# Input laid out turned for the start of a two-layer kernel, with contiguous weight blocks and more value tiles

## The chip, the cores and the metric

The kernel runs on one core of one Trainium2 chip. The metric is the device time of one execution in microseconds (us), as the median of several executions. The engines are TensorE (PE in the profile, PEld for its loading of weights), VectorE (DVE, `V` in the code), ScalarE (ACT, `S`), GpSimd (POOL, `G`) and SyncE (SP), which issues most of the DMA transfers (`nc.sync`). An engine name with a q behind it is that engine's sequencer.

## The reference

A batch of one, 256 tokens, width 2048, float32. A first layer (RWKV-7: five mixed inputs, four 2048x2048 products, a scan over 32 heads of 64, an output product), then a second (sparse attention with compressed, selected and window branches), each behind an rmsnorm, and a last norm. What the change touches is computed here:

```python
def rmsnorm(x, g):
    xf = x.astype(jnp.float32)
    y = xf * lax.rsqrt(jnp.mean(xf * xf, axis=-1, keepdims=True) + NORM_EPS)
    return (y * g.astype(jnp.float32)).astype(x.dtype)
...
    xx = token_shift(u) - u
    mixed = u[None] + xx[None] * mu[:, None, None, :]
    rkvz = jnp.einsum('nbtd,nde->nbte', mixed[:4], w_rkvz)
...
    def step(S, inp):
        r_t, w_t, k_t, v_t, a_t, b_t = inp
        sa = jnp.einsum('bhvk,bhk->bhv', S, a_t)
        S = S * w_t[:, :, None, :] + sa[..., None] * b_t[:, :, None, :] + v_t[..., None] * k_t[:, :, None, :]
        return S, jnp.einsum('bhvk,bhk->bhv', S, r_t)
```

Here u is the normed x of the first layer.

## The kernel before

**Precision and weights.** Each float32 operand of a large product is split into a high part and a low part (the rest), and three products make one. Weights arrive in pieces of 512 KB (`wraw`, five buffers, issued on SP in L179); ScalarE writes the high part (L213) and VectorE subtracts for the low part (L192), a few units ahead of TensorE (class `Weights`: `ensure`, `high`, `low`). While `W.hold` is set, low parts are written one at a time by `W.low(1)`. Weights for v, z and the outputs are loaded by rows of 512 columns or more (`rows`), those for r, k and the gate of the second layer by blocks of 128 columns (`cols128`, L293), whose rows in memory are 512 bytes long.

**Inputs.** The mixed inputs have the width on partitions: 16 blocks of 128 by 256 tokens. `xn` holds the normed x with a zero column ahead of the first token, `xx` the difference to the token before; `mixed_in` (L432) makes one mixed block of them on VectorE, `split_into` (L426) its high part on ScalarE and its low part on VectorE.

**Start (L346 to L505).** x is loaded on SP by tokens, two tiles of 128 tokens by 2048, in five pieces with three small parameter loads between them. ScalarE and VectorE square and sum them (`square`), VectorE and POOL make the reciprocal norm (`rstd0`), VectorE multiplies x by it (`scale`), TensorE turns the blocks (`turn_half`, `turn_x`), ScalarE multiplies by the gain and copies to `xn`, and VectorE or POOL makes `xx` (`norm_x`). The parameter rows are turned on TensorE as well. `keep_warm(n)` has TensorE multiply ones by ones, with no use of the result; `WARM` says how often at each place. `manual_schedule` holds the engines to the order of the program there. Blocks 2 to 15 are prepared by a generator (`prep`, `mixgen_v`), and another (`mixgen`) makes the inputs for w, a, z, k and r; both are pumped while the products run.

**Products of the first layer.** `phase_v` runs the v product and the two narrow products for w and a over all blocks, four blocks at a time; `store_v` (L626) copies its result through `vst` tiles on ScalarE and stores it to memory. Then come z, sixteen blocks of k with their own chain on all engines, and the inverse of small triangular matrices, made in pieces on VectorE, ScalarE and POOL (L822) and stored to `tnd` and `yvd`.

**Scan (L988 to L1545).** Eight pairs U of heads are worked through beside the r product and the first output products. A planner (`Deal`) lists every step with its engine, an estimated duration, what it needs and a lag, computes due times, and issues the steps in the order that it finds; `("at", n)` is a time of n us in its plan before which a step isn't placed. The engines and SP keep this order. Steps used here: `a` and `y` load pieces of the inverse (`load_a`, `load_y`, which fills `Yb`) on POOL's DMA queue; `v` loads the values into `uv`; `gb` loads the gain and bias of the group norm; `ars` are decay products on POOL; `G` (L1062) is the first PE step that needs `a` and `y` of a pair.

**Second layer.** `rstd` gives `RS`, the reciprocal norm per token; at the start of the attention it is spread over columns and turned into `RST` (L1754). `phase_q` splits turned queries into `qh` and `ql` (L1792, L1793).

## Time and profile before

| | us |
|---|---|
| median of 3 runs | 1132.98 |
| lowest and highest | 1128.69, 1133.59 |
| the profiled execution | 1135.73 |
| its span, first to last instruction | 1133.7 |
| TensorE busy in it | 1101.0 |
| VectorE busy | 860.5 |
| ScalarE busy | 713.5 |
| POOL busy | 378.0 |

The profile is of one execution. A row of its timeline has the start, the time taken, the engine, the line of the kernel, the operation, the tile written and the tiles read, the count, and in brackets the idle time before it with what ended it. A row of a group has line, engine, operation, tiles, shapes and count, then busy time and the mean in ns of one, then idle time before it and what ended that. A row of waits has who waited for whom, the sum, how often, and the longest. Matmuls are pipelined, so a busy TensorE need not be at its peak.

### The profile page before, as it was taken

Reading aid. Unit: us, or ns where it says so; the run is one execution under the profiler, and the core shown is the slowest. Engines: PE = TensorE matmul, PEld = TensorE weight load, DVE = VectorE, ACT = ScalarE, POOL = GpSimd, SP = SyncE. Lnnn points to the kernel's source line nnn. Section 1 sums busy time; section 2 is a strip of 40 time slices with the busy share of each in tenths; the row PEclk is TensorE's granted clock in tenths of the full one; section 3 lists DMA queues with packets and bytes.
Section 4 is the critical chain, followed back from the end, with each engine's and each line's share of the span. In section 5 each row is a group of like instructions: output and inputs, shape, how many; then the busy total and the mean of one; then the engine's idle time right before and its main releaser. Section 6 shows DMA issues by size and latency. Waiting matters only on the chain.

```text
span 1133.7 us, 24534 instructions
## 1 busy us (share of the span) xinstructions
PE 1101.0 (97%) x8880; PEld 935.3 (83%) x8880; DVE 860.5 (76%) x1783; ACT 713.5 (63%) x1700; POOL 378.0 (33%) x487
## 2 busy tenths in 40 slices
PE   7999999999999999999999999999999999999997
PEld 7778899987788777877788888787889988888786
DVE  6998976789869797677567776764576888988564
ACT  5667688867665356655556766664666666666553
POOL 1400057755384546661010010101334435362212
PEclk9999999999999999999999999999999999999999
DMA  6568888976999968865457658585645453848562
GB/s 221 172 194 221 246 220 245 258 204 210 263 293 273 229 159 244 201 186 156 133 177 250 205 167 290 164 282 167 188 146 159 124 140 102 210 120 276 160 190 104
DMA packets 239033, 225.35 MB, mean 199 GB/s; under 512 B 58053, under 2 KB 185333, under 8 KB 238912
## 3 DMA queue, kind: packets, MB, share of 16 engines
q1 hardware_dynamic: 233472, 216.65, 65.8%
q0 software_dynamic: 5440, 7.14, 2.3%
q8 instruction: 70, 1.15, 0.5%
q14 instruction: 51, 0.42, 0.1%
HBM read 200.48 MB, written 23.10 MB: 197 GB/s over the span
## 4 chain that ended last, share of the span: by engine, by line
PE 73%; DVE 13%; DMA 4%; issue 4%; ACT 3%; POOL 2%; SPq 0%; ACTq 0%; POOLq 0%; DVEq 0%
PE bank L589 11%; PE bank L591 11%; PE bank L588 11%; PE bank L1348 5%; DVE wlo L192 5%; PE bank L613 4%; PE bank L614 2%; PE bank L607 2%; PE bank L1351 2%; PE bank L244 2%; PE bank L608 2%; PE bank L609 2%; PE pair L1370 2%; ACT whi L213 1%; PE pair L1372 1%
## 5 line engine op out<-in xcount | busy, mean ns | idle before, releaser
L192 DVE TENSOR_TENSOR wlo<-wraw,whi 128x512 fp32r<-128x512 f32 (+2 forms) x616 | 444.3, 738 | 164.1 <-ACT whi L213 161.6
L213 ACT ACTIVATE whi<-wraw 128x512 fp32r<-128x512 f32 (+2 forms) x661 | 397.9, 619 | 221.4 <-PE bank L591 79.7
L589 PE MATMUL bank<-wlo,mx 128*128 128x512 f32 (+3 forms) x576 | 216.1, 377 | 3.6 <-DVE wlo L192 2.7
L591 PE MATMUL bank<-whi,mx 128*128 128x512 f32 (+3 forms) x576 | 214.2, 374 | 0.0
L588 PE MATMUL bank<-whi,mx 128*128 128x512 f32 (+3 forms) x576 | 186.9, 376 | 1.8 <-ACT mx L428 0.9
L589 PEld LDWEIGHTS bank<-wlo,mx 128*128 128x128 f32 x576 | 108.3, 188 | 22.7 <-DVE wlo L192 5.4
L588 PEld LDWEIGHTS bank<-whi,mx 128*128 128x128 f32 x576 | 107.6, 188 | 19.1 <-ACT mx L1937 1.2
L591 PEld LDWEIGHTS bank<-whi,mx 128*128 128x128 f32 x576 | 108.3, 188 | 16.3 <-POOL mx L1938 0.4
L1348 PE MATMUL bank<-mx,whi 128*128 128x512 f32 x256 | 102.1, 430 | 0.0
L192 POOL TENSOR_TENSOR wlo<-wraw,whi 128x512 fp32r<-128x512 f32 (+2 forms) x48 | 63.1, 1316 | 110.6 <-ACT whi L213 88.7
L613 PE MATMUL bank<-mx,whi 128*128 128x512 f32 x240 | 86.8, 398 | 0.0
L607 PE MATMUL bank<-mx,whi 128*128 128x256 f32 (+1 forms) x288 | 83.0, 288 | 0.3 <-ACT mx L428 0.3
L608 PE MATMUL bank<-mx,whi 128*128 128x256 f32 (+1 forms) x288 | 81.4, 283 | 0.0
L609 PE MATMUL bank<-mx,wlo 128*128 128x256 f32 (+1 forms) x288 | 81.3, 282 | 0.0
L589 PE MATMUL bank<-wlo,kvh 128*128 128x512 f32 x192 | 76.9, 401 | 0.0
L591 PE MATMUL bank<-whi,kvl 128*128 128x512 f32 x192 | 76.1, 396 | 0.0
L614 PE MATMUL bank<-mx,wlo 128*128 128x256 f32 x256 | 70.6, 285 | 0.2 <-DVE wlo L192 0.2
L1351 PE MATMUL bank<-mx,wlo 128*128 128x256 f32 x256 | 70.5, 283 | 0.0
L588 PE MATMUL bank<-whi,kvh 128*128 128x512 f32 x192 | 67.4, 395 | 0.0
L1348 PEld LDWEIGHTS bank<-mx,whi 128*128 128x128 f32 x256 | 47.9, 189 | 10.5
L607 PEld LDWEIGHTS bank<-mx,whi 128*128 128x128 f32 (+1 forms) x288 | 54.2, 188 | 1.3 <-ACT mx L428 0.7
L609 PEld LDWEIGHTS bank<-mx,wlo 128*128 128x128 f32 (+1 forms) x288 | 54.2, 188 | 0.8 <-DVE wlo L192 0.2
(365 smaller groups left out, 2303.9 us busy)
## 6 DMA issues: line engine op xcount, KB each, us to landing
wraw<-in_a_w_rkvz_dram SPq DMA_DIRECT2D x128, 512.0 KB, 5.5
wraw<-in_kv_w_dram SPq DMA_DIRECT2D x48, 512.0 KB, 4.5
wraw<-in_b_w_in_dram SPq DMA_DIRECT2D x40, 512.0 KB, 4.2
wraw<-in_a_w_o_dram SPq DMA_DIRECT2D x32, 512.0 KB, 4.6
wraw<-in_b_w_o_dram SPq DMA_DIRECT2D x32, 512.0 KB, 4.3
spd<-sp SPq DMA_DIRECT2D x16, 642.0 KB, 4.4
wraw<-in_b_w_in_dram SPq DMA_DIRECT2D x24, 384.0 KB, 3.4
spl<-spd SPq DMA_DIRECT2D x14, 642.0 KB, 7.4
```

Source lines behind the costliest of these rows:

```text
L192: eng.tensor_tensor(lv, src, hv.bitcast(F32), op=OP.subtract)
L213: self.nc.scalar.activation(hv, src, AF.Copy, **self.mark)
L588: PE.matmul(o, mh[:, ts], wh[:, 0, :], start=k == ends[0], stop=False)
L589: PE.matmul(o, mh[:, ts], wl[:, 0, :], start=False, stop=False)
L591: PE.matmul(o, ml[:, ts], wh[:, 0, :], start=False, stop=k == ends[1])
L607: PE.matmul(o, wh[:, s, :], mh, start=k == 0 and first, stop=False, **kw)
L608: PE.matmul(o, wh[:, s, :], ml, start=False, stop=False, **kw)
L609: PE.matmul(o, wl[:, s, :], mh, start=False, stop=k == NK - 1, **kw)
L613: PE.matmul(o, wh[:, s, :], joint[nm, k], start=k == 0, stop=False, **kw)
L614: PE.matmul(o[:, :T], wl[:, s, :], mh, start=False, stop=False, **kw)
L1348: both = lambda: PE.matmul(o, wh[:, s, :], joint["r", k], start=k == 0, stop=k == NK - 1)
L1351: PE.matmul(o[:, :T], wl[:, s, :], mixed["r", k][0], start=False, stop=False)
```

## The change

The host passes x already turned, as `turned_x` (16 blocks of 128 by 256 tokens), all parameter rows already turned in one array, the weights for r, k and the gate as contiguous blocks (4 KB for each partition instead of eight rows of 512 bytes), and gain and bias of the group norm in the order of their tile.

At the start, ScalarE and VectorE each square half of the blocks of every piece of x, and TensorE sums them over the width: the squares are its weights, a column of ones is the moving operand, two products for each block. POOL's power gives the reciprocal norm for each token; two products with the identity, whose weights are that column repeated 128 times, spread it over all partitions into `rst` in PSUM. One VectorE operation per block then makes `xn` from x, gain and `rst`. For blocks 0 and 1 the mix is made from `xn` directly; `xx` comes from POOL (`lag_x`). Turnings, scalings and ScalarE's copies go. Small ScalarE operations (`pace`) give the gains of later blocks, so that these follow ScalarE's order. From block 6 on the low part of the input a is written by POOL (`KG`). The warm-ups are 17, 3 after each piece but the last, 6 and 6.

Besides, `vst` has five buffers; `uv` has the time blocks of one head contiguous, so that its loads have rows of 1 KB; `gb` is loaded by 2 transfers instead of 8 each time; in the planner the `y` loads of pair 1 may start at 7 instead of 12 and those of pair 4 go to SP; `RST` is made before the key and value products instead of at the start of the attention; `qh` and `ql` get a higher priority; and the memory for POOL's DMA descriptors is set to 8 KB of each partition instead of the default.

```diff
-KS, KD = 3, 3
-WARM, PRE, KM, MEN = (17, 3, 1, 4), 4, 4, "vsgp"
+KD, KG = 3, 6
+WARM, KM, MEN = (17, 3, 6, 6), 4, "vsgp"
...
-PRI = dict(iv=-80, chPE=0, chE=100, srPE=0, srE=0, skPE=0, skE=0, stE=0, atPE=1000, atE=0, cpPE=0, w=0, mx=0)
+PRI = dict(ql=300, iv=-80, chPE=0, chE=100, srPE=0, srE=0, skPE=0, skE=0, stE=0, atPE=1000, atE=0, cpPE=0, w=0, mx=0)
...
-    def cols128(w, c0):
+    def cols128(blocks, j):
         for q in range(2):
-            W.add(by_rows(w, 8 * q, 8, c0, 128), 4)
+            W.add(blocks[j, q], 4)
...
-    def load_x(tt, c0, c1):
-        nc.sync.dma_start(xt[:, tt, c0:c1], a["x"][0, tt * 128:(tt + 1) * 128, c0:c1])
-
-    nc.sync.dma_start(cst[:, 0:128], a["blob"][:, 0:128])
-    load_x(0, 0, 1024)
-    load_x(0, 1024, 2048)
-    load_x(1, 0, 1024)
-    nc.sync.dma_start(prow[0:16, 0, :], g16(a["a_norm_g"][0]))
-    nc.sync.dma_start(prow[16:112, 0, :], a["a_mu"][0].rearrange("i (j p) -> (i j) p", p=128))
-    nc.sync.dma_start(prow[112:128, 0, :], g16(a["a_k_k"][0]))
-    load_x(1, 1024, 1536)
-    load_x(1, 1536, 2048)
+    prm = consts.tile([128, 2, 128], F32, name="prm")
+
+    XK = ((0, 4), (4, 8), (8, 12), (12, 14), (14, 16))
+    S.dma_start(prm.rearrange("p a b -> p (a b)"), a["rows"])
+    S.dma_start(cst[:, 0:128], a["blob"][:, 0:128])
+    for k0, k1 in XK:
+        nc.sync.dma_start(xt[:, k0:k1, :], a["turned_x"][:, k0:k1, :])
...
-        V.tensor_tensor(l, src, h.bitcast(F32), op=OP.subtract)
+        (G if nm == "a" and k >= KG else V).tensor_tensor(l, src, h.bitcast(F32), op=OP.subtract)
...
-    def scale(tt, c0, c1):
-        sl = xt[:, tt, c0:c1]
-        V.tensor_scalar(sl, sl, rs[:, tt, 1:2], None, op0=OP.mult)
-
-    def norm_x(k, px, eng):
-        S.activation(xn[:, k, 1:], px, AF.Copy, scale=G_A[:, k:k + 1])
-        eng.tensor_tensor(xx[:, k, :], xn[:, k, 0:T], xn[:, k, 1:], op=OP.subtract)
-
+    sums, rst = accp("sums")[:, 0:2], accp("rst")[:, :T]
+
+    def norm_x(k, gain):
+        V.scalar_tensor_tensor(xn[:, k, 1:], xt[:, k, :], gain, rst, op0=OP.mult, op1=OP.mult)
+
+    def lag_x(k):
+        G.tensor_tensor(xx[:, k, :], xn[:, k, 0:T], xn[:, k, 1:], op=OP.subtract)
...
-        turned_x = [accp("tp") for _ in range(2)]
-        S.activation(sq[:, 0:1], half[:, 0:1], AF.Square)
+        S.activation(g1[:, 0:1], half[:, 0:1], AF.Square)
         keep_warm(WARM[0])
-        square(0, 0, 1024, 0, S)
-        square(0, 1024, 1536, 1, V)
-        square(0, 1536, 2048, 2, V)
-        rstd0(0)
-        square(1, 0, 1024, 0, S)
-        square(1, 1024, 1536, 1, V)
-        scale(0, 0, 512)
-        for kp in range(2):
-            turn_half(turned_x, 0, kp)
-        keep_warm(WARM[1])
-        square(1, 1536, 1792, 2, V)
-        square(1, 1792, 2048, 3, S)
-        PE.transpose(pp[:, 0:128], prow[:, 0, :], ident)
+        for n, (k0, k1) in enumerate(XK):
+            mid = (k0 + k1) // 2
+            squares = [ph0.tile([128, 2, T], F32, name=nm, bufs=2) for nm in ("sqs", "sqv")]
+            S.activation(squares[0][:, :mid - k0], xt[:, k0:mid], AF.Square)
+            V.tensor_tensor(squares[1][:, :k1 - mid], xt[:, mid:k1], xt[:, mid:k1], op=OP.mult)
+            for k in range(k0, k1):
+                sl = squares[k >= mid][:, (k - k0) % (mid - k0)]
+                for tt in range(2):
+                    PE.matmul(sums[:, tt:tt + 1], sl[:, tt * 128:tt * 128 + 128], ones[:, 0:1], start=k == 0 and tt == 0,
+                              stop=k == NK - 1, skip_group_check=True)
+            if n + 1 < len(XK):
+                keep_warm(WARM[1])
+            if n == 1:
+                S.activation(g1, MU[2][:, 0:2], AF.Copy, scale=-1.0, bias=1.0)
+        V.tensor_scalar(rs[:, 0, :], sums, 1.0 / D, 1e-6, op0=OP.mult, op1=OP.add)
+        G.tensor_tensor(rs[:, 1, :], rs[:, 0, :], half[:, 0:2], op=OP.pow)
         keep_warm(WARM[2])
-        rstd0(1)
+        for tt in range(2):
+            PE.matmul(rst[:, tt * 128:tt * 128 + 128], rs[:, 1, tt:tt + 1].to_broadcast([128, 128]), ident, start=True, stop=True)
+        keep_warm(WARM[3])
         W.hold = True
-        W.ensure(PRE)
-        scale(1, 0, 256)
-        V.tensor_copy(prm0, pp[:, 0:128])
-        turn_half(turned_x, 1, 0)
-        keep_warm(WARM[3])
-        W.low(1)
-        scale(1, 256, 512)
-        turn_half(turned_x, 1, 1)
-        px = turned_x[0]
+        W.ensure(2)
         for k in range(2):
-            norm_x(k, px[:, 256 * k:256 * k + 256], V)
-            m = mixed_in("v", k)
+            norm_x(k, G_A[:, k:k + 1])
+        for k in range(2):
+            m = ph1.tile([128, T], F32, name="mtmp", bufs=3)
+            S.activation(m, xn[:, k, 1:], AF.Copy, scale=g1[:, k:k + 1])
             W.low(1)
+            V.scalar_tensor_tensor(m, xn[:, k, 0:T], MU[2][:, k:k + 1], m, op0=OP.mult, op1=OP.add)
             split_into(m, "v", k)
+            W.ensure(3 + k)
         W.hold = False
 
     def prep(kp):
-        if kp == 2:
-            banks(tp=(6,))
-        px = turned_x[kp] if kp < 2 else turn_x(kp)
-        for i in range(2) if kp else ():
-            k = 2 * kp + i
-            sl = px[:, i * 256:i * 256 + 256]
-            norm_x(k, sl, G)
+        pace = ph1.tile([128, 3], F32, name="pace", bufs=1)
+        S.activation(pace[:, 0:2], G_A[:, 2 * kp:2 * kp + 2], AF.Copy)
+        S.activation(pace[:, 2:3], half[:, 0:1], AF.Copy, scale=0.0, bias=1.0)
+        for i in range(2):
+            norm_x(2 * kp + i, pace[:, i:i + 1])
+            lag_x(2 * kp + i)
+        W.mark = dict(scale=pace[:, 2:3])
+        for k in (0, 1) if kp == 1 else ():
+            lag_x(k)
...
-            t = ph0.tile([128, 512], F32, name="vst", bufs=2)
+            t = ph0.tile([128, 512], F32, name="vst", bufs=5)
...
-        for x, h in each:
-            for i, v in enumerate((a["a_ln_g"][0], a["a_ln_b"][0])):
-                src = bass.AP(tensor=v.tensor, offset=v.offset + U * 256 + x * 128 + h * 64, ap=[[0, 64], [256, NK // 4], [1, 64]])
-                nc.sync.dma_start(gb[H(x, h), i, x::2], src)
+        src = a["ln"]
+        for i in range(2):
+            nc.sync.dma_start(gb[R[i]].rearrange("p a b c -> p (a b c)"),
+                              bass.AP(tensor=src.tensor, offset=src.offset + (U // 4 * 2 + i) * 1024, ap=[[0, 64], [1, 1024]]))
...
-                add(("y", U, x, h), "G", 1120.0, lambda U=U, x=x, h=h: load_y(U, G, [(x, h)]), later("p", U - 3, 3, 1),
-                    ("yz", U) if U < 3 else None, ("at", 12 * min(U, 2)), ("yvd1",) if U == 4 else None, lag=5500.0)
+                add(("y", U, x, h), *(("Q", 950.0) if U == 4 else ("G", 1120.0)),
+                    lambda U=U, x=x, h=h: load_y(U, nc.sync if U == 4 else G, [(x, h)]), later("p", U - 3, 3, 1),
+                    ("yz", U) if U < 3 else None, ("at", (7, 24)[U > 1]), ("yvd1",) if U == 4 else None, lag=5500.0)
...
-            add(("gb", U), "Q", 3600.0, lambda U=U: load_gb(U), ("at", 22), *[later(k, U - 1, x) for k in "gb" for x in range(2)], lag=3000.0)
+            add(("gb", U), "Q", 900.0, lambda U=U: load_gb(U), ("at", 22), *[later(k, U - 1, x) for k in "gb" for x in range(2)], lag=3000.0)
...
+    def turn_rs():
+        pr = accp("tp")
+        for tt in range(2):
+            rb = bp.tile([128, 128], F32, name="rb", bufs=1)
+            V.tensor_copy(rb, RS[tt].to_broadcast([128, 128]))
+            PE.transpose(pr[:, tt * 128:(tt + 1) * 128], rb, ident)
+        V.tensor_copy(RST, pr[:, :T])
...
-            S.activation(qh, pt, AF.Copy)
-            V.tensor_tensor(ql, pt, qh.bitcast(F32), op=OP.subtract)
+            with tc.high_priority(offset=PRI["ql"]):
+                S.activation(qh, pt, AF.Copy)
+                V.tensor_tensor(ql, pt, qh.bitcast(F32), op=OP.subtract)
...
+def _laid(v):
+    col = lambda n: np.asarray(v[n], np.float32).reshape(-1, 128).T
+    blocks = lambda w: np.asarray(w, np.float32).reshape(2, 8, 128, 16, 128).transpose(3, 0, 2, 1, 4)
+    rows = [col(n) for n in ("a_norm_g", "a_mu", "a_k_k", "a_w0", "a_a0", "a_k_a", "a_r_k", "kv_norm_g", "b_norm_g")]
+    ln = [np.asarray(v[n], np.float32).reshape(2, 4, 2, 2, 64) for n in ("a_ln_g", "a_ln_b")]
+    half = lambda p: [np.stack([t[:, :, x, p ^ x] for x in range(2)], 2) for t in ln]
+    turned_x = np.asarray(v["x"][0], np.float32).T.reshape(16, 128, T).transpose(1, 0, 2)
+    return {"turned_x": turned_x, "rows": np.concatenate(rows + [np.zeros((128, 256 - 16 * 14), np.float32)], 1),
+            "ln": np.stack([np.stack(half(p), 1) for p in range(2)], 1),
+            "wr": blocks(v["a_w_rkvz"][0, 0]), "wk": blocks(v["a_w_rkvz"][0, 1]), "wg": blocks(v["b_w_in"][0][:, 2096:4144])}
...
-    nc = _bacc.Bacc("TRN2", target_bir_lowering=False, num_devices=1)
+    nc = _bacc.Bacc("TRN2", target_bir_lowering=False, num_devices=1, dynamic_dma_scratch_size=8192)
```

More of the change, by code (lines that the diff above doesn't have):

```diff
@@ L270, in accp @@
         return psum.tile([128, 512], F32, name=f"bank{b[n % len(b)]}", bufs=1)
-    banks(acc=(0, 1, 2, 3, 4, 5), tp=(6, 7), lora=(7,), warm=(0,), pp=(5,))
+    banks(acc=(0, 1, 2, 3, 4, 5), lora=(7,), warm=(0,), rst=(6,), sums=(7,))
     vd = dram.tile([NK, 128, T], F32, name="vd")
@@ L284, in hybrid_kernel @@
     win = a["b_w_in"][0]
-    wr, wk, wv, wz = [a["a_w_rkvz"][0, i] for i in range(4)]
+    wv, wz = [a["a_w_rkvz"][0, i] for i in (2, 3)]
     def by_rows(w, k0, nk, c0, cols):
@@ L379, in hybrid_kernel @@
     G.memset(ones, 1.0)
-    V.memset(prow[96:, 1, :], 0.0)
     half = consts.tile([128, 16], F32, name="half")
     G.memset(half, -0.5)
-    sq = ph0.tile([128, 1024], F32, name="sqs")
-    sqv = ph0.tile([128, 512], F32, name="sqv")
-    ss = ph0.tile([128, 2, 4], F32, name="ss")
     rs = ph0.tile([128, 2, 2], F32, name="rs")
-    prm = consts.tile([128, 2, 128], F32, name="prm")
     prm0, prm1 = prm[:, 0, :], prm[:, 1, :]
@@ L439, in mix @@
         split_into(mixed_in(nm, k), nm, k)
-    def turn_x(kp):
-        px = accp("tp")
-        for tt in range(2):
-            for i in range(2):
-                PE.transpose(px[:, i * 256 + tt * 128:i * 256 + tt * 128 + 128],
-                             xt[:, tt, (2 * kp + i) * 128:(2 * kp + i + 1) * 128], ident)
-        return px
     warm = accp("warm")[:, :128]
-    pp = accp("pp")
     def keep_warm(n):
@@ L535, in mixgen_v @@
             if k == KM:
+                scaled_params()
                 startup.close()
-            if k == KS:
-                for i in range(1, 4):
-                    for tt in range(2):
-                        scale(tt, 512 * i, 512 * i + 512)
             if k % 2 == 0:
@@ L995, in hybrid_kernel @@
     Yb.extend(one(f"Yb{i}", [128, 2, NCH, 64]) for i in (1, 2))
-    UV = [one(f"uv{i}", [128, 2, NCH, 2, 64]) for i in range(2)]
+    UV = [one(f"uv{i}", [128, 2, 2, NCH, 64]) for i in range(2)]
     AMA = [one(f"ama{i}", [128, 2, NCH, 64]) for i in range(2)]
@@ L1120, in removal @@
         for x, h in each:
-            PE.matmul(px[H(x, h), x], AMA[U % 2][:, x, c, :], uv[:, x, c, h, :], start=True, **mm)
+            PE.matmul(px[H(x, h), x], AMA[U % 2][:, x, c, :], uv[:, x, h, c, :], start=True, **mm)
     def bonus(U):
@@ L1645, in hybrid_kernel @@
     cmpx = {}
+    turn_rs()
     def kv_k(which, t):
@@ L2054 @@
         args[name] = nc.dram_tensor(f"in_{name}_dram", v.shape, mybir.dt.from_np(v.dtype), kind="ExternalInput").ap()
+    for name, v in _laid(inputs).items():
+        arrays[f"in_{name}_dram"] = np.ascontiguousarray(v)
+        args[name] = nc.dram_tensor(f"in_{name}_dram", v.shape, F32, kind="ExternalInput").ap()
     arrays["in_blob_dram"] = BLOB
```

55 lines of the change are left out of this document (14 added, 41 removed).

## The prediction

> **What bounds the kernel now.** I read the page's busy shares first, then the table by stage, then the list of what TensorE (PE) waits for, then the timeline of the first 20 us.
>
> ```profile
> span 1133.7 us, 24534 instructions
> PE 1101.0 (97%) x8880; PEld 935.3 (83%) x8880; DVE 860.5 (76%) x1783; ACT 713.5 (63%) x1700; POOL 378.0 (33%) x487
> ...
> 0.00:30.00 30.00, 24.32 (x123) 21.34 (x124) 20.82 (x51) 15.33 (x32) 5.42 (x15) 0.94 0.67 225
> 100.00:200.00 100.00, 100.00 (x699) 90.25 (x698) 80.29 (x163) 78.78 (x189) 37.13 (x44) 1.00 0.88 240
> 1100.00:1134.00 34.00, 25.26 (x202) 24.50 (x200) 16.51 (x30) 13.06 (x30) 5.90 (x6) 0.95 0.32 110
> ```
>
> The columns of a stage are its length and then busy time of PE, PE's weight loads, VectorE (DVE), ScalarE (ACT) and GpSimd (POOL), then the granted clock. PE is idle for 33 of 1133.7 us, and 14.4 of these lie in the first 30 us (5.7) and the last 34 us (8.7). The change touches nothing in the last 34 us. So time comes only from PE's waits in the first stage, from the few waits between, and from work that PE no longer does. These are the waits that the change touches:
>
> ```profile
> PE pair L1062 <- DMA Yb<-yvd: 4.1, 2, 2.5
> PE bank L458 <- DVE xt L463: 3.8, 1, 3.8
> PE bank L244 <- DVE ql L1793: 0.6, 1, 0.6
> PE bank L1789 <- DVE ql L1793: 0.6, 1, 0.6
> PE bank L1759 <- DVE rb L1758: 0.5, 1, 0.5
> ```
>
> **Start-up.** Before, x comes in by rows; VectorE and ScalarE square and sum it, and PE only turns it. Afterwards PE adds up the squares.
>
> ```profile
> 1.00 5.48 PE L454 MATMUL bank<-ones 128*128 128x128 f32 x34 [1.00 <-POOL half L382]
> 1.19 1.37 SPq L360 DMA_DIRECT2D xt<-in_x_dram  x3
> 5.66 1.06 ACT L401 ACTIVATE sqs<-xt 128x1024 f32<-128x1024 f32 x1 [3.42 <-DMA xt<-in_x_dram]
> 10.03 0.42 ACT L401 ACTIVATE sqs<-xt 128x256 f32<-128x256 f32 x1 [0.57 <-DMA xt<-in_x_dram]
> 10.84 0.15 DVE L407 TENSOR_SCALAR rs<-rs 128x1 f32<-128x1 f32 x1
> 11.07 0.55 POOL L408 TENSOR_TENSOR rs<-rs,half 128x1 f32<-128x1 f32 x1 [1.56 <-DVE rs L407]
> 15.78 0.50 PE L588 MATMUL bank<-whi,mx 128*128 128x512 f32 x1 [0.90 <-ACT mx L428]
> ...
> 240.18 0.52 PEld L740 LDWEIGHTS bank<-cst,t 128*128 128x128 f32 x4 [0.68 <-ACT t L732]
> 240.62 0.19 PEld L607 LDWEIGHTS bank<-mx,whi 128*128 128x128 f32 x1
> ...
> L740 PE MATMUL bank<-cst,t x64: 169/251/272, 151.7 to 279.6; 128*128 128x2 f32 x64
> ```
>
> The last piece of x is there at 10.0 us, and the first real product starts at 15.78. The new sums are 32 float32 products, each with a 128x128 block of squares as weights and one moving column. The nearest row is L740, with two moving columns. Its 32 products show as 64 passes, two each. Four passes take from 240.18 to 240.62, so one costs 0.11 us whatever the column count, since each reloads the weights. The 17 opening warm-ups are 34 passes and hold PE till about 6.4 us. Behind them PE now has, in its queue's order, 64 passes of sums and 4 x 3 warm-ups (24 passes): 88 x 0.11 = 9.7 us. The first piece of x is there at about 5.5 us and two blocks take ScalarE some 0.6 us to square (1.06 for four), so PE is never short of squares. Its end is 6.4 + 9.7 + 0.2 for the last result = 16.3 us, long after x is complete. That x is asked for earlier (three small parameter loads leave SP's queue between the pieces) is therefore worth nothing.
>
> From there one step waits for the next: VectorE's scale 0.15 and POOL's power 0.55, with 0.1 between each, to 17.2. Meanwhile PE has six warm-ups (12 passes, to 17.6), then spreads the norm with two products (4 passes, 0.44, and 0.25 to the result): 18.3. VectorE has two norms at 0.48 (row L1597 below), one low part of weights at 0.69 and the mix at 0.48, to 20.4. ScalarE's high part takes 0.42, as any 256 columns there. The first real product starts at 20.8: **+5.0 us**. ScalarE's g1 product and the two weight splits lie beside the sums. Bounds: nothing below -0.3 (were the sums free, x at about 9.5 and the same chain of some 6 us give 15.5), above +7.5 (the clock, see the rivals).
>
> **Products of v, 16 to 100 us.**
>
> ```profile
> 16.00:60.00 44.00, 42.13 (x208) 34.02 (x208) 42.47 (x88) 28.37 (x67) 15.14 (x14) 1.00 0.51 157
> 60.00:100.00 40.00, 40.00 (x208) 33.88 (x207) 39.84 (x95) 27.82 (x61) 0.00 (x0) 1.00 0.64 196
> ...
> L192 DVE TENSOR_TENSOR wlo<-wraw,whi 128x512 fp32r<-128x512 f32 x51 | 34.2, 686 | 0.2 <-ACT whi L213 0.2
> L429 DVE TENSOR_TENSOR mx<-mtmp,mx 128x256 fp32r<-128x256 f32 x55 | 23.3, 441 | 0.5 <-ACT mx L428 0.5
> L463 DVE TENSOR_SCALAR xt<-xt,rs 128x512 f32<-128x512 f32 x6 | 2.5, 476 | 0.0
> ...
> L467 POOL TENSOR_TENSOR xx<-xn 128x256 f32<-128x256 f32 x14 | 15.1, 1100 | 28.3 <-ACT xn L466 28.3
> ...
> L1597 DVE SCALAR_TENSOR_TENSOR kvl<-bank,prm,kvh 128x256 fp32r<-128x256 f32 x16 | 7.4, 479 | 1.7 <-ACT kvh L1596 1.7
> ...
> L445 PE MATMUL bank<-cst,xt 128*128 128x128 f32 x24 | 3.6, 272 | 0.0
> ...
> 235.41 0.90 DVE L759 TENSOR_TENSOR sp<-nk,sp 128x256 f32<-128x256 f32 x1
> 244.81 0.42 DVE L759 TENSOR_TENSOR sp<-nk,sp 128x256 f32<-128x256 f32 x1
> ```
>
> VectorE is full throughout, so here it, not PE, sets the pace until about 60 us. Its account: 14 more norms on PSUM at 0.48 are +6.7; six scalings at 0.48, one copy of 0.3 and one difference of 0.4 go, -3.6; ten low parts of a move to POOL, 10 x 0.44 = -4.4. That is -1.3. Against it, POOL gets ten more operations of 1.1 us, and the two rows of L759 show one VectorE operation at 0.90 beside POOL's work and 0.42 at another time; if each of the ten costs between 0 and 0.48, the account lies between -1.3 and +3.5. I take **0**, near the row L429 whose mean is only slightly stretched. The 24 turnings that PE loses (3.6 us) and ScalarE's 14 fewer copies (it gets 14 tiny ones, the pace, instead) buy nothing while VectorE is full; were PE the bound they would be worth up to -3.6. POOL's low parts of a queue its later differences behind them, and VectorE's mixes wait for those; POOL was idle for two thirds of 16 to 60, so I charge nothing.
>
> More value tiles: ScalarE's wait for them goes, but PE stood still in none of it (100.0 of 100 us busy): 0.
>
> ```profile
> ACT vst L629 <- DMA vd<-vst: 2.8, 1, 2.8
> ACT whi L213 <- DMA wraw<-in_a_w_rkvz_dram: 10.3, 8, 2.0
> ```
>
> Long rows for wr, wk and wg relieve the 10.3 us of the second row, which PE's list of waits doesn't show either: **0**, between -2 and 0 since PE's other waits of 200 to 300 us may shorten.
>
> **The scan, 345 to 580 us.** The two waits for Yb are those of pairs 1 and 4.
>
> ```profile
> 355.78 2.23 POOL L939 DMA_DIRECT2D Yb<-yvd  x4
> ...
> 362.36 0.55 POOL L931 DMA_DIRECT2D a<-abd  x1 [1.36 <-DMA Yb<-yvd]
> 366.74 1.18 POOL L939 DMA_DIRECT2D Yb<-yvd  x2 [1.75 <-DMA a<-abd]
> ...
> 372.00:376.00 4.00, 1.54 (x43) 1.18 (x43) 3.88 (x7) 1.39 (x5) 1.19 (x3) 1.00 1.30 133
> 376.00:380.00 4.00, 4.00 (x44) 3.20 (x37) 0.15 (x1) 1.51 (x5) 1.80 (x3) 0.57 0.41 81
> ...
> 434.98 1.09 POOL L939 DMA_DIRECT2D Yb<-yvd  x2 [0.56 <-DMA yvd<-invX]
> ...
> 445.57 0.55 POOL L939 DMA_DIRECT2D Yb<-yvd  x1 [0.34 <-PE pair L1144]
> ```
>
> POOL issues the loads of pair 1 from 355.78 and stands still at 362.36 and 366.74 until older loads have landed; the last comes after PE needs it. The plan now lets these loads start 5 us earlier, in POOL's idle time ahead of 353: the wait of 2.5 us goes. They then stand before POOL's decay products on its queue, a delay of some 2 us for a step that PE reaches about 10 us later. Right behind the wait the granted clock is 0.57 for 4 us of full PE: 4 x 0.43 = 1.7 us, which goes with it. For pair 4 eight loads move from POOL to SP. POOL took from 434.98, when yvd had landed, to 445.57 over them and the loads between; SP can issue the eight in a row, at 0.46 each as for x (1.37 for three), so the 1.6 us of the second wait go. Weights queue behind them on SP, some 4 us later, within the pieces that are loaded ahead. Sum **-5.8**, between -5.8 and 0. The new layout of uv, the fewer gb loads and the other size of the memory for POOL's descriptors touch no wait in PE's list: 0.
>
> [...]
>
> **Attention.** The norm is turned earlier, beside dense products: -0.5. High priority for ql can save two waits of 0.6, but pushes weight splits back on the same two engines: -0.6, between -1.2 and +1.2.
>
> **Sum:** +5.0 + 0 + 0 - 5.8 - 0.5 - 0.6 = **-1.9 us**. The profiled execution took 1135.73 us (span 1133.7 and 2.0 around it), 2.7 above the median 1132.98 of the runs shown; I take the difference off the median: **1131.1 us**.
>
> **Rivals.** (a) The sums are hidden: if a pass with one column costs half or less, or a block needs one pass, x sets the pace and the start comes out at -0.3 instead of +5.0: 1132.98 - 7.2 = 1125.8. Against it stands L740, the same form but for one column. Chance 0.20.
> (b) Slower: the clock. One-column passes use PE little; if they count as idle, the clock is halved from about 10.8 us, as it was before after 6.4 to 10.3 us of idle PE. It decides if it falls before the sums end. Of the 88 passes 48 are then left, 48 x 0.11 = 5.3 us more, and 16 further passes of warm-up and spreading 1.8, less the 0.4 that POOL covers, and up to 1.7 on the first products: +7.5 by the middle: 1131.1 + 7.5 = 1138.6. For it speaks the half clock after the old start; against it that warm-ups lie between. Chance 0.14. [...]
> (c) The waits in the scan stay: eight outstanding loads and their 6 to 8 us, not the planned start, set the last landing, or SP stands before yvd as it holds the weights. Then -5.8 is lost: 1136.9. The stops at 362.36 and 366.74 speak for it. Chance 0.18.
> (d) The change does what it says but VectorE loses to POOL, +3.5: 1134.6. Chance 0.06.
> My forecast has the rest, 0.42.
>
> ```profile
> 10.80:14.20 3.40, 3.40 (x19) 3.40 (x18) 1.74 (x7) 2.56 (x6) 0.55 (x1) 0.50 1.03 364
> ```
>
> **How the numbers follow.** A measurement of this kernel tells about 0.5% (5.7 us) from no change: faster is below 1127.3, slower above 1138.6. Faster: most of (a), 0.17, and 0.11 from the forecast with the -2 and -3.6 of its bounds. Slower: half of (b), 0.07, a fifth of (c), 0.04, and 0.01 of (d). The rest, 0.60, is within. The range takes in (a) with its lower half cut, (c), (d) and (b) to its price: 1123.5 to 1138.5.
>
> **What would show it.** Right: L740-like passes of about 0.11 us back to back till 16 us; the first real product near 20.8; no wait for Yb above 0.5 us and a clock of 1.0 at 370 to 380 plus the shift; VectorE full to 100 us. Wrong: PE waiting for squares between 7 and 10 us (then (a)); a clock of 0.5 before 20 us (then (b)); a new wait of PE in the scan (then (c)).

## The result, and the profile after

The changed kernel is slower: 1143.53 us (1141.58 to 1147.46, four runs) beside 1133.28 (1128.69 to 1135.64, four runs) for the kernel before; the ratio is 1.0111, with a 95% interval of 1.0085 to 1.0138, that is some 10 to 16 us. I had forecast 1131.1, between 1123.5 and 1138.5. The profiled execution of after has a span of 1142.0 us.

The page of after, its span and the first row of busy shares:

```profile
span 1142.0 us, 24643 instructions
PE 1113.2 (97%) x8946; PEld 943.8 (83%) x8946; DVE 863.5 (76%) x1770; ACT 712.3 (62%) x1700; POOL 383.0 (34%) x489
```

PE is as full as before, only for longer: 1113.2 us of work in place of 1101.0. So the time didn't go into waits that this row would show. The table by stage tells more (columns as in the prediction; the second and third row are the stretches between two changes of the granted clock):

```profile
0.00:30.00 30.00, 28.43 (x176) 26.86 (x176) 11.18 (x23) 9.82 (x23) 3.11 (x13) 0.89 0.53 188
15.60:22.40 6.80, 6.80 (x34) 6.80 (x34) 1.04 (x4) 0.37 (x1) 0.71 (x1) 0.50 0.03 11
254.50:257.90 3.40, 3.40 (x18) 3.40 (x17) 3.30 (x10) 1.74 (x6) 2.23 (x3) 0.50 0.78 207
100.00:200.00 100.00, 98.41 (x632) 86.00 (x631) 86.05 (x174) 77.63 (x180) 29.90 (x37) 1.00 0.81 238
```

In the first 30 us PE is busy for 28.4 us instead of 24.3, and for 6.8 us of it at half its clock. From 100 to 200 us, where it never stood still before, it loses 1.6 us. The timeline of PE at the start of after:

```profile
0.99 6.11 PE L418 MATMUL bank<-ones 128*128 128x128 f32 x34 [0.99 <-POOL half L373]
6.95 0.95 PE L442 MATMUL bank<-ones,sqs 128*128 128x1 f32 x8
7.76 1.03 PE L442 MATMUL bank<-ones,sqv 128*128 128x1 f32 x8
8.65 0.91 PE L418 MATMUL bank<-ones 128*128 128x128 f32 x6
...
16.15 0.85 PE L442 MATMUL bank<-ones,sqs 128*128 128x1 f32 x4
16.86 0.99 PE L442 MATMUL bank<-ones,sqv 128*128 128x1 f32 x4
17.72 2.91 PE L418 MATMUL bank<-ones 128*128 128x128 f32 x12
20.42 1.06 PE L452 MATMUL bank<-cst,rs 128*128 128x128 f32 x4
21.27 2.05 PE L418 MATMUL bank<-ones 128*128 128x128 f32 x12
23.89 0.50 PE L544 MATMUL bank<-whi,mx 128*128 128x512 f32 x1 [0.57 <-ACT mx L402]
```

Eight passes of sums take 0.81 to 0.89 us from start to start (6.95, 7.76, 8.65), without a gap: 0.10 to 0.11 each, and no wait for squares. From 15.6 us on a pass takes longer: four from 16.15 to 16.86 take 0.71, 0.18 each. The first real product starts at 23.89 us, 8.1 later than before.

To see where the rest goes I laid the products of two traces side by side, matched by line and shape, and took the difference of their starts against the kernel before. This **shift** is 8.1 us at the first real product, 12.1 at 170 us (the v product and its neighbours are done), 13.3 at 320 us, 7.8 at 560 us (behind the scan) and 8.4 at the end. The waits of PE that answer to those of before are:

```profile
PE bank L564 <- DVE mx L403: 1.7, 2, 1.3
PE bank L544 <- ACT mx L402: 1.4, 2, 0.8
PE pair L1018 <- DMA Yb<-yvd: 0.8, 1, 0.8
PE bank L244 <- DVE ql L1755: 0.6, 1, 0.6
PE bank L1750 <- DVE ql L1755: 0.6, 1, 0.6
```

Of the two waits for Yb one is left; those for ql are as they were; the wait for `rb` is gone. New is the wait for the low part of a mix (L403); that for the high part (L402), 0.9 us before, has grown to 1.4.

### The profile page after: what moved, and what is told of

The parts are those of the page before. It is cut to its first block, busy times and chain, and to the rows that moved or that the text cites. A ratio compares the mean times of both kernels' runs of the same rounds, so it can differ in the third digit from the quotient of the medians.

```text
span 1142.0 us, 24643 instructions
## 1 busy us (share of the span) xinstructions
PE 1113.2 (97%) x8946; PEld 943.8 (83%) x8946; DVE 863.5 (76%) x1770; ACT 712.3 (62%) x1700; POOL 383.0 (34%) x489
## 4 chain that ended last, share of the span: by engine, by line
PE 68%; DVE 18%; issue 5%; DMA 4%; ACT 3%; POOL 1%; SPq 0%; ACTq 0%; POOLq 0%; DVEq 0%
PE bank L545 9%; PE bank L544 9%; PE bank L547 9%; DVE wlo L192 7%; PE bank L1304 5%; PE bank L569 4%; PE bank L1307 2%; PE bank L570 2%; PE bank L244 2%; DVE mtmp L409 2%; PE bank L563 2%; PE bank L564 2%; PE bank L565 2%; PE pair L1326 2%; DVE mx L403 1%
```

## The experiments

A ratio is against runs of the kernel before on the same chip (its medians there: 1131.0 to 1132.3). "Shift" always compares with the one profile of before. **Growth** is the shift at 170 us less that at the first real product: what the stage of the v product costs. First product, growth and scan are read from one profiled execution of each run, the median and the ratio from all its runs.

| run | first product | growth | scan (560 less 320 us) | median | ratio, interval |
|---|---|---|---|---|---|
| before | 15.78 | 0 | 0 | | 1 |
| after | 23.89 | +4.0 | -5.6 | 1143.53 | 1.0111 (1.0085 to 1.0138) |
| wide | 21.64 | +4.1 | -6.2 | 1138.07 | 1.0060 (1.0043 to 1.0077) |
| onepass | 15.53 | +4.6 | -4.8 | 1134.19 | 1.0018 (1.0002 to 1.0034) |
| newplus | 18.67 | +3.8 | -5.2 | 1134.92 | 1.0021 (1.0005 to 1.0036) |
| alow | 21.78 | +0.7 | -6.4 | 1136.11 | 1.0043 (1.0029 to 1.0057) |
| kg2 | 21.98 | +3.9 | -0.2 | 1140.57 | 1.0082 (1.0049 to 1.0114) |
| twonorm | 20.49 | +10.6 | -4.7 | 1146.77 | 1.0134 (1.0109 to 1.0159) |
| widekg16 | 21.54 | +8.9 | -6.0 | 1145.20 | 1.0126 (1.0101 to 1.0150) |
| kg16 | 26.62 | +8.4 | -2.5 | 1150.47 | 1.0169 (1.0148 to 1.0191) |
| vst2 | 26.75 | +3.4 | -7.7 | 1142.57 | 1.0103 (1.0082 to 1.0124) |
| oldstart | 15.59 | -0.2 | -2.9 | 1130.13 | 0.9984 (0.9967 to 1.0001) |
| oldrows | 15.29 | -0.2 | -6.1 | 1129.61 | 0.9981 (0.9962 to 1.0001) |
| oldkg | 16.11 | +4.6 | -4.3 | 1134.49 | 1.0030 (1.0012 to 1.0047) |
| oldplus | 15.37 | +4.1 | -6.3 | 1133.31 | 1.0011 (0.9996 to 1.0025) |
| oldbest | 15.39 | +3.6 | -4.0 | 1133.40 | 1.0014 (0.9998 to 1.0030) |
| yonly | 15.43 | -0.2 | -1.6 | 1132.49 | 1.0002 (0.9986 to 1.0017) |

### The start of before with the rest of the change (oldstart)

In place of the new start stands the old one (`xt` by tokens, `square`, `scale`, `turn_x`, two `vst` tiles, no `KG`); wr, wk and wg blocks, uv, gb, the `y` loads, RST, ql and the descriptor memory are those of the change.

> The start of the kernel before (turning, squares summed by VectorE and ScalarE, two value tiles), with all the rest of the change: long rows, the scan's loads, RST, ql. Theory: the loss of the changed kernel is made in the first 140 us (start +8.1, value stores on SP's queue +3), and the scan gains 5.5: first real product at 15.8, shift against the kernel before 0 at 300 us and -5.5 from 545 us on, 1127.8 us. Rival: part of the loss between 100 and 290 us comes from the long rows (or the smaller memory for descriptors): shift +2 to +5 at 290 us and 1130 to 1133 us.

The ratio is 0.9984 where that of after is 1.0111: 1.3% or 14 us. The shift is -0.4 at 170 us, -0.8 at 320 and -3.8 at 560. The whole loss therefore lies in the new start and what belongs to it (norms, POOL's low parts), and the long rows cost nothing. The scan's gain is smaller than I expected, and the median is only 0.9 us below that of before (1131.04).

### Sums with 128 columns (wide)

```diff
-    sums, rst = accp("sums")[:, 0:2], accp("rst")[:, :T]
+    sums, rst = accp("sums")[:, :T], accp("rst")[:, :T]
-    PE.matmul(sums[:, tt:tt + 1], sl[...], ones[:, 0:1], ...)
+    PE.matmul(sums[:, tt * 128:tt * 128 + 128], sl[...], ones, ...)
```

> The changed kernel with the column of ones widened to 128 columns in the sums: as many passes with as many weight loads, every column of the result the same, one of them used. Clock theory: it is the single moving column that counts as an idle TensorE; then a pass still takes about 0.11 us, the granted clock stays 1.0 from 6 to 25 us, the 6.8 us at half clock go, and the first real product comes 3 to 3.4 us earlier, near 20.7 instead of 23.9; 1140.3 us. Rival: the clock falls because of something else (the short stops between the pieces, the warm-ups): half clock stays at about 15.6 us, first product at 23.9, 1143.5 us. Second rival: a pass with 128 columns takes longer than its weight load (0.2 us): sums 6 us longer, first product at 27 or later.

The timeline of PE of this run:

```profile
7.42 1.06 PE L442 MATMUL bank<-ones,sqs 128*128 128x128 f32 x8
8.31 1.06 PE L442 MATMUL bank<-ones,sqv 128*128 128x128 f32 x8
...
17.25 1.50 PE L418 MATMUL bank<-ones 128*128 128x128 f32 x12
18.59 0.65 PE L452 MATMUL bank<-cst,rs 128*128 128x128 f32 x4
...
21.64 0.50 PE L544 MATMUL bank<-whi,mx 128*128 128x512 f32 x1 [1.07 <-ACT mx L402]
```

and its row by stage for the stretch that had half the clock in after:

```profile
15.60:22.40 6.80, 5.73 (x48) 5.45 (x47) 2.81 (x7) 1.73 (x4) 0.71 (x1) 1.00 0.01 2
```

A pass costs the same 0.11 us (8.31 less 7.42, by eight) with 128 columns as with one, and yet the clock stays at 1.0 until the last 5 us of the kernel (its mean over the span is 0.998, in after 0.994). So it was the one-column products, not the short stops or the warm-ups, that let the clock fall. One profile alone could be chance, but alow, kg2, twonorm and widekg16 below have the same wide sums and no half clock before their first product either, which comes at 20.49 to 21.98, and all three profiles with one-column sums (after, vst2, kg16) have it (first product at 23.89, 26.75 and 26.62). By the ratios the run is 0.5% (5.8 us) below after; in the profiles 2.25 us of it are at the start, less than the 3 to 3.4 that I expected. How long the half clock lasts differs between executions: 6.8 us from 15.6 in after, 10.2 us in the runs vst2 and kg16, which begin alike. The row of vst2 by stage:

```profile
13.70:23.90 10.20, 10.20 (x49) 10.20 (x49) 0.58 (x2) 1.39 (x3) 0.71 (x1) 0.50 0.14 53
```

There the first product starts at 26.75.

### One pass for a sum (onepass)

```diff
-WARM, KM, MEN = (17, 3, 6, 6), 4, "vsgp"
+WARM, KM, MEN = (13, 1, 6, 6), 4, "vsgp"
+    onr = ph0.tile([128, 128], F32R, name="onr")
+    G.tensor_copy(onr, ones)
-    squares = [ph0.tile([128, 2, T], F32, name=nm, bufs=2) ...]
+    squares = [ph0.tile([128, 2, T], F32R, name=nm, bufs=2) ...]
```

> The kernel with the widened sums, and besides: the squares are written in the rounded form fp32r, so that a sum is one pass instead of two (32 in place of 64), and there are 13 warm-ups ahead and one after each piece instead of 17 and 3. My theory of the start: passes of 0.11 us back to back set the end of the sums. 26 passes end near 6 us, and x (complete at 9.55 us) sets the pace: sums end near 10.3, then the same chain as in the run with widened sums (17.25 to 21.64, 4.4 us): first real product at 14.7 instead of 21.64, 7 us earlier; if all of it lasts, 1131 us. Rival: the weights (pieces landed at 10.75, 12.1 and 13.7 us) or the high parts on ScalarE take over as what the first product waits for: first product at 16.5 to 18, 1133 to 1134.5 us. If the clock falls in the waits for x, 1 to 3 us more.

The timeline of onepass, with a row of POOL and two of PE's weight loads (PEld) between those of PE:

```profile
8.83 0.52 PEld L444 LDWEIGHTS bank<-onr,sqs 128*128 128x128 f32 x4 [0.22 <-ACT sqs L439]
...
10.90 0.39 PE L444 MATMUL bank<-onr,sqv 128*128 128x128 f32 x2
...
11.63 0.71 POOL L451 TENSOR_TENSOR rs<-rs,half 128x2 f32<-128x2 f32 x1 [10.33 <-DVE rs L450]
12.40 0.53 PEld L454 LDWEIGHTS bank<-cst,rs 128*128 128x128 f32 x4
...
15.53 0.50 PE L546 MATMUL bank<-whi,mx 128*128 128x512 f32 x1 [1.07 <-ACT mx L404]
```

Now PE waits for squares (0.22 <-ACT sqs), the sums end at 11.1 instead of 17.25, and the first product starts at 15.53, 6.1 us earlier than in wide, if not at the 14.7 that I expected. The passes were the bound of the start. But that only draws level with before (15.78): the chain behind the sums is as long as what it replaced. The 4.6 us of growth stay, and the median is 2.4 us above that of before.

### Low parts of a left out (alow), norms doubled (twonorm), more low parts on POOL (kg2)

All three are edits of wide.

```diff
 alow
-        (G if nm == "a" and k >= KG else V).tensor_tensor(l, src, h.bitcast(F32), op=OP.subtract)
+        if nm == "a" and k >= KG:
+            S.activation(l, src, AF.Copy)
+        else:
+            V.tensor_tensor(l, src, h.bitcast(F32), op=OP.subtract)
 twonorm
-            norm_x(2 * kp + i, pace[:, i:i + 1])
+            for _ in range(2):
+                norm_x(2 * kp + i, pace[:, i:i + 1])
 kg2
-KD, KG = 3, 6
+KD, KG = 3, 2
```

> The kernel with the widened sums; the ten low parts of the input a that POOL writes are left out (ScalarE writes a copy of the value in their place, so the output is another one). VectorE and POOL both lose them. Contention theory: POOL's ten operations of 1.3 us stretch VectorE's (mix 0.541 us instead of 0.508, low part of weights 0.695 instead of 0.672); without them the waits of TensorE between 22 and 165 us fall from 6.8 us to about the 2.8 of before, the shift against the kernel before at 165 us from 9.9 to 6, 1134 us. Rival (the load is VectorE's own, the 14 norms): mean durations and shift stay, 1138 us.

> The kernel with the widened sums; each of the 14 norms of blocks 2 to 15 on VectorE is made twice (0.47 us each, 6.6 us more; the output is the same). If VectorE alone sets the pace from 22 to 165 us: shift at 165 us grows by 5 to 6.6, 1143 to 1144.6 us. If the norms lie beside TensorE's work as I took it (account 0): within 1 us of 1138.

> The kernel with the widened sums; POOL writes the low parts of a from block 2 on (14 instead of 10). If an operation moved is worth its 0.44 us on VectorE less a third for the stretch: 1 us less at 165 us, 1137 us. If the stretch takes it all: 1138 us. If POOL's queue becomes late for the differences that the mixes need: more than 1 us longer, 1139 to 1140 us.

twonorm: growth 10.6 against 4.1, 6.5 more. The 14 added norms are 6.6 us by their length, 5.5 by the 0.39 from start to start that is read below, and half clock for 3.4 us at 41.5 us is in the 6.5 too. So VectorE sets the pace of this stage, and added work there costs about its full price. The median, 1146.77, is above the 1143 to 1144.6 that I expected; there is a second half clock at 382.8 us. alow: growth 0.7; without POOL's ten operations 3.4 of the 4.1 us are gone, and the median, 1136.11, lies between the two that I expected. They don't cost this by being late: VectorE waits for POOL's low parts 0.6 us in all from 24 to 143 us, in after and in wide. To see why, two timelines of VectorE, first of after, then of alow:

```profile
77.15 0.68 DVE L192 TENSOR_TENSOR wlo<-wraw,whi 128x512 fp32r<-128x512 f32 x1
77.75 1.75 DVE L409 SCALAR_TENSOR_TENSOR mtmp<-xx,prm,xn 128x256 f32<-128x256 f32 x3
79.43 1.28 DVE L192 TENSOR_TENSOR wlo<-wraw,whi 128x512 fp32r<-128x512 f32 x2
```

```profile
78.55 0.69 DVE L192 TENSOR_TENSOR wlo<-wraw,whi 128x512 fp32r<-128x512 f32 x1
79.15 1.27 DVE L412 SCALAR_TENSOR_TENSOR mtmp<-xx,prm,xn 128x256 f32<-128x256 f32 x3
```

Three mixes take 1.75 us where POOL is at work, 1.27 where it isn't. What POOL did just then in after:

```profile
77.35 1.09 POOL L403 TENSOR_TENSOR mx<-mtmp,mx 128x256 fp32r<-128x256 f32 x1 [2.07 <-ACT mx L402]
```

It is not a general slowing down: nearly every low part on POOL makes one operation of VectorE take 0.49 us longer (a mix 0.96 in place of 0.47), and the others are as fast as alone. Added up over the stage, VectorE's operations are held up by 4.6 us in before (by POOL's 14 differences), 8.4 in after and in wide, 3.9 in alow. The norms (L423), which read one operand from PSUM, are not held up: the 14 from 27.5 to 53.2 us, where POOL makes its differences, take 0.47 to 0.48 us each, and the two of blocks 0 and 1, at 21.5 us with POOL idle, 0.48. The mix, which reads both its tiles from SBUF, takes 0.96 beside a low part, 0.83 beside a difference (at 35.11 us) and 0.47 alone. That the operand in PSUM makes the difference is my reading of these rows; no run tests it alone.

The groups of after from 24 to 143 us (busy us, mean ns, idle before):

```profile
L192 DVE TENSOR_TENSOR wlo<-wraw,whi 128x512 fp32r<-128x512 f32 (+1 forms) x80 | 54.9, 696 | 2.7 <-ACT whi L213 2.6
L409 DVE SCALAR_TENSOR_TENSOR mtmp<-xx,prm,xn 128x256 f32<-128x256 f32 x71 | 37.4, 541 | 0.7 <-POOL mx L403 0.6
...
L403 POOL TENSOR_TENSOR mx<-mtmp,mx 128x256 fp32r<-128x256 f32 x10 | 13.1, 1307 | 36.2 <-ACT mx L402 33.1 <-PE bank L547 3.1
...
L423 DVE SCALAR_TENSOR_TENSOR xn<-xt,pace,bank 128x256 f32<-128x256 f32 x14 | 6.0, 471 | 0.3 <-ACT pace L469 0.3
```

Back to back VectorE starts a new operation before the last has ended (in after a mix at 68.46, a low part at 68.86, the next mix at 69.19): a low part of a costs 0.335 us from start to start, a norm or mix 0.39, though they show as 0.41 and 0.47. With these the account of the stage is: 14 norms +5.5, six scalings and three small copies -2.9, ten low parts -3.4, new small parameter operations +0.6, held up +3.8 (8.4 less 4.6). Sum +3.6, measured +4.1.

kg2 (four more low parts on POOL) leaves the growth at 3.9: a further operation on POOL gains about nothing. Its scan has waits that wide doesn't have, and half clock at 461 us, and its four runs lie at 1137.1, 1137.8, 1143.4 and 1145.0, so its median says nothing on this.

### The low parts, and the parameters, taken apart (kg16, widekg16, oldplus, oldkg, oldrows)

kg16 and widekg16 set `KG = 16` (no low part on POOL) in after and in wide. oldplus adds to oldstart the turned parameters (loaded on ScalarE's queue, no `prow`) and ten low parts of a on POOL; oldkg and oldrows have one of the two each.

```diff
 oldplus, oldkg
-        V.tensor_tensor(l, src, h.bitcast(F32), op=OP.subtract)
+        (G if nm == "a" and k >= 6 else V).tensor_tensor(l, src, h.bitcast(F32), op=OP.subtract)
 oldplus, oldrows
-    nc.sync.dma_start(prow[0:16, 0, :], g16(a["a_norm_g"][0]))
...
+    S.dma_start(prm.rearrange("p a b -> p (a b)"), a["rows"])
```

> The changed kernel with the ten low parts of the input a on VectorE again instead of POOL. If VectorE sets the pace from 24 to 140 us and POOL's work beside it costs nothing: 10 x 0.44 = 4.4 us more by 140 us, 1147.9 us. If POOL's work stretches VectorE's operations by as much as it takes over (my step, net 0 with the 14 norms): no change, 1143.5 us.

> The kernel with the start of before and the rest of the change (run oldstart), and besides the parameters already turned, loaded on ScalarE's queue (no small loads between the pieces of x, no turning and copying of them), and ten low parts of a on POOL. Turned parameters: x complete 0.5 us earlier, first product at 15.1 instead of 15.6. VectorE's account: 4.4 us less, of which the stretch by POOL takes more than half back; TensorE's waits between 22 and 165 us, 2.8 us, fall to 1 to 2. Sum 1 to 2 us below the run oldstart: 1128.5 to 1129. Rival: the first product waits for weights, and POOL's late differences cost what VectorE saves: 1130 to 1131.

> The run oldstart with one edit more: POOL writes the ten low parts of a from block 6 on. The stage is the time from the first real product to the wait at the first products of k (132.9 us in oldstart, 137.0 in oldplus, which had this edit and the turned parameters). If POOL's operations cost VectorE as much as they take off it (10 x 0.5 us against 10 x 0.335): stage 134 to 137 us, 1131.5 to 1134 us. If the turned parameters made oldplus longer: stage 131 to 133, 1129 to 1130.

> The run oldstart with the parameters already turned and loaded on ScalarE's queue, nothing else. If the low parts on POOL made oldplus longer: first product near 15.2, stage 132.5 to 133.5, 1129.5 to 1130. If the turned parameters did it (VectorE's order of low parts and mixes changes, and mixes for k come late): stage 135 to 137 with a stop of PE at 146 to 151 us as in oldbest, 1132 to 1134.

> The kernel with the widened sums (stage 137.1 us, no half clock) with the ten low parts of a on VectorE. By the durations from start to start: 10 x 0.335 more on VectorE and 10 x 0.49 less stretch, stage 135.5 us, 1136.5 us. If the order decides as in the run kg16 (141.4, with 2.5 of it from half clock at 163.6): stage 138.5 to 141, 1140 to 1142 us.

The same ten low parts on POOL make the stage 4.8 us longer with the old start (growth 4.6 in oldkg, -0.2 in oldstart), and 4.8 shorter with the new one (4.1 in wide, 8.9 in widekg16; 4.0 in after, 8.4 in kg16). The parameters do nothing of the kind (oldrows -0.2). In oldkg nine of POOL's ten operations hold up a mix; the sum of what is held up is 9.5 us against 4.5 in oldstart. So there +5.0 stand against 10 x 0.335 = 3.4 that VectorE is spared: 1.6 of the 4.8 follow from this account. oldplus, with both edits, is at 1133.31, later than either of my expectations, and so is kg16.

In widekg16 the account would give -0.7 (3.4 more work, 4.1 less held up), and up to the first product of k the kernel does go that way. This product in wide, then in widekg16:

```profile
149.74 0.28 PE L563 MATMUL bank<-mx,whi 128*128 128x256 f32 x1
```

```profile
146.82 0.28 PE L563 MATMUL bank<-mx,whi 128*128 128x256 f32 x1
```

It starts 128.1 us behind the first real product in wide and 125.3 in widekg16, 128.0 in after and 125.4 in kg16, 125.1 in alow, 124.7 before. So up to there, through the products of v and the first ones of z, the ten low parts on POOL cost 2.7 to 2.8 us with the new start too. What turns the sum round comes behind: in widekg16 PE runs ahead to 154.6 us and then stops at the first products of k, whose mixes aren't ready; its list of waits from 150 to 165 us, and its row by stage behind the stop:

```profile
PE bank L564 <- DVE mx L403: 3.7, 3, 2.7
```

```profile
159.70:166.50 6.80, 6.17 (x24) 5.34 (x24) 3.28 (x6) 2.91 (x7) 1.82 (x3) 0.50 0.32 87
```

Behind the stop the clock is at half for 6.8 us. In kg16 it is the same, 3.4 us of waits and half clock for 6.8 us from 163.6. Wide and after wait only 0.5 us at this place. Why the mixes of k are ready so late in those two runs stays open; that the order of low parts and mixes on VectorE decides it is a guess.

### One version to beat both (newplus, oldbest), the value tiles (vst2), the y loads alone (yonly)

newplus is onepass with ScalarE multiplying the gain into x, so that VectorE norms two blocks in one operation, a low part of weights moved behind the first mix, four warm-ups ahead of the spreading, and two value tiles. oldbest is oldrows with all differences xx on VectorE. vst2 is after with two value tiles, yonly is before with the two edits of the `y` loads alone.

```diff
 newplus
...
-        for i in range(2):
-            norm_x(2 * kp + i, pace[:, i:i + 1])
+        V.tensor_tensor(xn[:, 2 * kp:2 * kp + 2, 1:], xt[:, 2 * kp:2 * kp + 2, :], ..., op=OP.mult)
 oldbest
-            norm_x(k, sl, G)
+            norm_x(k, sl, V)
 vst2
-            t = ph0.tile([128, 512], F32, name="vst", bufs=5)
+            t = ph0.tile([128, 512], F32, name="vst", bufs=2)
```

> The kernel with sums in one pass (run onepass), two value tiles, and besides: the gain of a block is multiplied into x by ScalarE, so that VectorE norms two blocks in one operation (7 of about 0.7 us instead of 14 of 0.47: 1.7 us less); four warm-ups instead of six ahead of the spreading; the low part of the weights behind the first mix instead of ahead of it (0.68 us). VectorE theory: first product at 14.8 instead of 15.53, shift against the kernel before at 165 us 1.5 to 2 instead of 4.3: 1131 to 1132 us. Rival: ScalarE's 14 products of 0.42 us delay the high parts of the weights: shift stays at 4, 1133 to 1134 us.

> The run oldplus without its low parts of a on POOL, and with the 14 differences xx of blocks 2 to 15 on VectorE too, so that POOL does nothing beside VectorE from 16 to 130 us. Lock theory: each of POOL's operations holds up one VectorE operation with two operands in SBUF by 0.4 to 0.5 us (mix 0.47 alone, 0.83 beside xx, 0.96 beside a low part), while VectorE needs only 0.335 us from start to start for the operation itself; so every mix takes 0.47, the stage from the first product to the first products of k is 0 to 1.5 us shorter than in run oldstart (132.9 us) and 4 to 5.5 shorter than in oldplus (137.0), and the time is 1128.5 to 1130. Rival (the 4 us of oldplus come from the turned parameters or from other waits): stage 135 to 137 us, 1132 to 1133.

> The changed kernel with two value tiles again instead of five. Queue theory: with five tiles SP issues eight value stores in a row (112.3 to 118.1 us) and the next weight piece is asked for only then, so that ScalarE waits 3.4 us for weights at 120.6 and TensorE loses about 3 us between 117 and 161 us; with two tiles weight loads stand between the stores again, and the shift against the kernel before stays near 9 at 140 us instead of 12.1: 1140.5 us. Rival: VectorE, full to 140 us, sets the pace there, and the stores don't matter: shift 12 at 140 us, 1143.5 us.

> The kernel before with one edit of the change alone: the planner's loads of Yb (pair 1 may start at 7 instead of 12, pair 4 on SP). My step of the scan: both waits for Yb go, 2.5 and 1.6 us, and with the first the 3.4 us of half clock behind it (1.7 us): shift -5.8 at 545 us. By the runs so far the wait of pair 4 comes back as 0 to 1.4 us and other waits of 0.8 to 1 us arise: shift -3 to -5.5 at 545 us, 1126 to 1129 us. Rival: the gain in the scan comes from the other edits (uv, gb): shift 0 to -1.

newplus: misses. Four of ScalarE's new gain products (7.44 to 9.15 us) stand ahead of its third piece of squares, PE waits 0.88 us for these at 9.72 us, the clock is at half from 10.7 us for 6.8, and the first product comes at 18.67. In onepass the same squares start 0.9 us earlier and the clock is 1.0 there; that PE's wait lets it fall fits this, but no run tests it alone. The growth fell only from 4.6 to 3.8.

oldbest: every mix takes 0.47 us, as the lock theory has it, but PE runs ahead and stops at 146 to 151 us for the mixes of k, with half clock for 6.8 us behind it, as in widekg16. Up to the first product of k the stage is 3.0 us shorter than in oldstart (121.6 and 124.6 us), behind the stop it is longer, growth 3.6: the expectation held for the operations and failed for the stage.

vst2: growth 3.4 instead of 4.0, a ratio lower by 0.0008 (0.9 us), with intervals that overlap. SP's timeline of after does show the queue that I suspected, eight value stores in a row and the next weights only at 118.1:

```profile
112.33 5.68 SPq L281 DMA_DIRECT2D vd<-vst  x8
118.11 2.72 SPq L179 DMA_DIRECT2D wraw<-in_a_w_rkvz_dram  x4
```

It is worth at most 0.6 us of the growth, not 3; that theory fell.

yonly: no wait for Yb is left in PE's list, and where the old profile had half clock (376 to 380 us) it is 1.0. Its list from 340 to 560 us has other waits in their place ("issue" is time in which PE waited for nothing that the profile shows):

```profile
PE pair L1141 <- issue: 1.7, 1, 1.7
PE pair L1141 <- DVE sta L1178: 1.0, 1, 1.0
PE pair L1121 <- issue: 0.8, 1, 0.8
```

Behind the first of them the clock is at half for 3.4 us (from 503.5). The shift over the scan is -1.6, and the median is that of before (ratio 0.9986 to 1.0017). The gain that the profile promised is not there in the median.

oldrows is the lowest of all: 0.9981, between 0.9962 and 1.0001. It keeps the old start and takes the turned parameters, the long rows, and the scan, RST and ql edits. That is 2 us, and not clearly below before.

## Why the prediction was wrong

By the ratio the change costs 12.6 us where I forecast a gain of 1.9. In the terms of the forecast the start is 3.1 us worse, the products of v 4.0, and the scan and all behind it 5.1 (-1.8 in place of -6.9); 1.2 is a half clock that I didn't forecast. That is 13.4 of the 14.5.

**Start, forecast +5.0; measured +8.1 in the profile.** The mechanism was right: 88 passes of 0.11 us (0.10 to 0.11 measured), with x long there. In wide, at full clock, the sums end at 17.25 (forecast 16.3, the warm-ups having ended 1 us later) and the chain behind them takes 4.4 us (forecast 4.5): 5.9 in all. The other 2.25 us are the half clock, rival (b), whose mechanism was right and whose place was wrong: it begins at 15.6 us, not at 10.8, so that it catches the last sums, the warm-ups and the spreading instead of 48 passes. In other executions it begins at 13.4 to 13.7 and costs some 5 us (26.62 and 26.75). Rival (a) named the way out, one pass for a block, and onepass shows its size: -6.1 against wide. Level with the old start it is, but not ahead.

**Products of v, forecast 0; measured +4.0.** This step failed in its price. I had the account and its bounds (-1.3 to +3.5), with each of POOL's ten operations costing VectorE between 0 and 0.48 us, and took the middle because the mean of L429 was only slightly stretched. But a mean over many operations alone and few beside POOL says nothing of those few: each holds up one operation for 0.49, the upper end. The row of L759 with 0.90 beside 0.42, which I quoted, was the price. And I counted the low part that is spared at 0.44, its length, where 0.335 from start to start is what VectorE gets back. The rival for it, (d), had +3.5 and a chance of 0.06. With the measured prices the account gives +3.6, and the stage up to the first product of k is 3.3 longer in after; 0.7 more comes at the start of k. Not all of it is understood: the same account gives 1.6 of the 4.8 us that the ten operations cost in oldkg and 0.7 of the 2.8 in wide, and with them back on VectorE the kernel is some 7 us slower yet (kg16, widekg16), by the stop at k.

**The scan, forecast -5.8; in the profiles -5.6, in the median about 0 to -2.** The profile of after seems to bear it out. But yonly, with this edit alone, is where before is, and oldstart, with all edits but the start, 0.9984. The waits that went were those of one execution, 1135.73 us, 3 to 5 above the medians of before beside the experiments. The same scan gains between 0.2 and 7.7 us in the profiles of the table, as waits of 1 to 2 us and half clocks behind them fall here or there. What failed is the step from one execution's waits to the median. The mechanism held for pair 1, whose wait is in no profile of a kernel with the new plan; that for pair 4 is back in six of the ten profiles with the new start, with 2.4 us in kg2. Rival (c), that the waits stay, is right in that part only.

**Half clock at 254.5 us, not forecast.** Between 170 and 320 us the shift grows by 1.2 in after; PE waits at 249.8 to 253.5 and runs 3.4 us at half clock behind. In wide this is absent (0.0), in alow, onepass, yonly and oldbest a half clock falls between 240 and 256 us too. It comes with the old start too (yonly, oldbest), so I take it for scatter and no part of the change.

**Long rows 0, value tiles 0, ql and RST -1.1.** The first two hold (oldstart, vst2). From 560 us to 1100 the shift moves by 0.2 in after: the wait for `rb` is gone, but so small that nothing is to be seen, and the waits for ql stay at 0.6 each. The -1.1 is not there.

The sum: by the ratios after is 14 us above oldstart, and 8.1 + 4.0 + 1.2 = 13.3 is what the profile of after finds in the first 320 us. The rest of the change is worth 0.16% of 1131 us, -1.8 (oldstart against before, interval -3.7 to +0.1).
